# A transformer block in split float32 on one core: weight parts moved in the on-chip memory, and the products of the down-projection reordered

## The chip, the core and the metric

The kernel runs on one core of a Trainium2 chip. The core has TensorE (PE, matrix products, with its weight loads shown as PEld), VectorE (DVE), ScalarE (ACT), GpSimd (POOL) and SyncE (SP, which only issues DMAs). Each engine works off its own instructions in the order in which they were written into the program; between engines there are semaphores. The metric is the time of one execution in microseconds (us), the median of several runs.

## The reference, cut to what matters

One block over 512 tokens of width 2048. All weights and activations are float32.

```python
h    = rmsnorm(x, g_attn_pre)
proj = h @ w_in                               # q, k, v of 8 stick-breaking heads, latents of 8 MLA heads
o_sb, o_mla = stick_breaking(q, k, v), mla(latents, rope(positions))
x    = x + rmsnorm(concat(rmsnorm(o_sb), rmsnorm(o_mla)) @ w_o, g_attn_post)
h    = rmsnorm(x, g_ffn_pre)
u    = causal_depthwise_conv(h @ w_up)        # w_up 2048 x 11264, width 3
gate, val = split(u)
x    = x + rmsnorm((gelu(gate) * val) @ w_down, g_ffn_post)   # w_down 5632 x 2048
```

## The kernel before, in words

**Split products.** A float32 product is made from three products of rounded parts: each factor is split into a high part (a rounding cast, `hi`, made on ScalarE) and a low part (what is left, `lo`, a subtraction on VectorE), and `three` issues high by high, high by low and low by high. Weights go the same way: a raw tile `wr` is loaded by SP, ScalarE casts it to `wh`, VectorE subtracts to `wl` (L109 and L111 in the attention, `w_parts`, L921, in the feed-forward).

**Start.** `gen_v` (L305) makes the values first: for each block of weight rows it loads weights (`load_w`), loads and splits a block of x, and issues 12 matmuls a block. The first two blocks are loaded one at a time, the others in pairs, into two raw buffers. On VectorE the operations of `rope_tables` (the angles, sine and cosine by range reduction, L390 to L425) lie between those splits. Then comes the first query and key product, `qk0`; after 6 of its matmuls `bcast` (L145) spreads the row scales over the partitions with a float32 matmul of `t` (VectorE, L139) by `ones`.

**Feed-forward.** The columns of gate and value are taken in 22 units of 256 pairs. Unit 0 is done plainly (`plain_part`, L865). The other 21 use a scheme of seven products in place of eight on a 2 x 2 split of weights and activations (`sevenfold`): p1 loads the quarter w11, p5 needs w11 + w12 (an addition in place, `plus`, L925), p6 that + w22, p7 w12 + w22, p2 is w21, p3 w22, p4 w11 + w12 + w22 + w21. Each product of the up-projection is 48 matmuls of 256 columns (L984), 21 x 7 x 48 = 7056 in all. The parts have three buffers each (`w_pair`), the raw quarters four.

**Down-projection.** The 5632 rows of w_down go in five chunks of 1024 rows (four units), and the last 512 rows plainly (`last_steps`). A chunk has two halves of columns (q = 0, 1), and each half seven products of 24 matmuls of 512 columns (L1156), 5.4 us each. The left sides, sums of the gated activations split in two parts, are made by `g_side` (L1123 on ScalarE, L1124 and L1129 on VectorE): those of the next chunk product by product in the half q = 1, those of the first chunk at the end of the up-projection (`then`). In the traces the sides go by their pages: product 1 reads a6h, 2 a6l, 5 a3h, 6 s, 7 a3l, 3 and 4 act_lo. Products 1 and 2 share two PSUM banks X, 5 and 3 share D, 7 and 4 share C, 6 has Y. After product 1, X is added to the accumulator u2 (`add_to`, L1094; in the first chunk a copy on ScalarE, L1092), then product 2 adds on in X, and the sum goes to the accumulator "11". For p7 and p4 the raw sums are made by DMAs of GpSimd that accumulate (`added`). After the last chunk twelve operations combine the accumulators (L1219, L1223, L1224), and the plain rows are added to them bank by bank (`take`, L1243).

**What sets the order.** The main loop keeps two products' weights ahead: it makes the parts of the product after next, then issues a product. `ORDER` (L1159) and the order in which `sevenfold` returns its parts set the products of a half. A scheduler lays the operations of each engine out from that, and `issue_after` holds one back behind another. A pool of tiles takes addresses from a stack; a tile that takes the address of an older one waits for the older one's last reader.

Of the kernel before, what the change touches and what calls it, by code (L numbers as in the profile page):

```python
# [19 lines left out]
P = 128  # L20
# [29 lines left out]
def hymba_block(ctx, tc, x, xT, positions, vecs, taps, w_in, w_uq, w_ukv, w_o, g_attn_post, w_up, w_down,  # L50
# [22 lines left out]

    ident = const.tile([P, P], F32, name="ident")
# [3 lines left out]
    ones = const.tile([P, P], F32, name="ones")  # L78
    po.memset(ones, 1.0)
# [25 lines left out]
    def load_w(src, r0, kn, c0, cols):  # L105
        raw = new_raw([P, kn, cols])
# [198 lines left out]
    def gen_v(vb, first=False):  # L305
        banks = [bank() for _ in range(NT)]
        steps = [1, 1] + [2] * 7 if first else [2] * 8
        for kg, kn in enumerate(steps):
            k0 = sum(steps[:kg])
            wh, wl = load_w(w_in, k0 * P, kn, 2 * SBW + vb * 512, 512)  # L310
# [12 lines left out]
        for t in range(NT):  # L323
            hi, lo = pg_v(R32), pg_v(R32)
            sc.activation(hi, banks[t], AF.Copy, scale=rx[:, t:t + 1])
            ve.scalar_tensor_tensor(lo, banks[t], rx[:, t:t + 1], f(hi), ALU.mult, ALU.subtract)
            v_sb[vb].append((hi, lo))
# [54 lines left out]
    def rope_tables():  # L382
# [6 lines left out]
        with behind(("lo", 4)):  # L389
# [100 lines left out]
    run(qk0, 1.0)  # L490
# [423 lines left out]
    made = []  # L914

# [12 lines left out]
    def sevenfold(quarter, shape, added=None):  # L928
# [3 lines left out]
        def p1():  # L932
            pair = w_pair(*shape)
            if not made:
                wq.tile([P, 256], F32, tag="gap", name="gap", bufs=1)
# [30 lines left out]
        if added:  # L966
            return p1, p2, p5, p6, p7, p3, p4
# [22 lines left out]
    def up_steps(unit):  # L990
# [61 lines left out]
        def then(use, *ns):  # L1052
            def both(w):
                use(w)
                if ns[0] == 6:
# [6 lines left out]
        if unit == NFF // 2 - 1:  # L1062
            return zip(sevenfold(quarter, (8, 256)), (m1, m5, then(m6, 1), then(m7, 2), m2, then(m3, 5),
                                            then(m4, 6, 7, 3, 4)))
# [14 lines left out]
    def open_down():  # L1079
        some(len(later))  # L1080
        tp_stack.close()
        d["gp"], d["gpool"] = stacked("gp", side="right")
        d["rest"] = kept("act_lo", (16, S), R32)
# [75 lines left out]
    ORDER = (1, 2, 5, 6, 7, 3, 4)  # L1159

    def down_steps(ch, q):
# [16 lines left out]
        def use(n, w):  # L1178
# [5 lines left out]
            if q == 1 and ch + 1 < NST:  # L1184
                g_side(ch + 1, n)
            if n == 1:
# [18 lines left out]
    def open_last():  # L1205
# [9 lines left out]
        for t in range(2):  # L1215
            for q in range(2):
                y[t, q], u2 = acc["11"][t, q], acc["u2"][t, q]
                y[2 + t, q], y[t, 2 + q], y[2 + t, 2 + q] = acc["21"][t, q], acc["12"][t, q], acc["22"][t, q]
                ve.tensor_tensor(y[t, 2 + q], y[t, 2 + q], u2, ALU.subtract)  # L1219
        for t in range(2):  # L1220
            for q in range(2):
                u2 = acc["u2"][t, q]
                ve.tensor_tensor(y[2 + t, 2 + q], y[2 + t, 2 + q], u2, ALU.subtract)  # L1223
                ve.tensor_tensor(y[2 + t, q], y[2 + t, q], u2, ALU.add)  # L1224
# [132 lines left out]
```

## Time and profile before

| | us |
|---|---|
| median of 3 runs | 2044.94 (2043.98 to 2048.38) |
| profiled execution | 2040.72 |
| its span (first to last instruction) | 2038.9 |
| TensorE busy | 2003.2 |
| VectorE busy | 1532.6 |
| ScalarE busy | 924.4 |

The profile is of one execution. It lists what each engine was busy with, and for each idle stretch what ended it. Busy time of TensorE is 98% of the span, so the stretches of interest are those between its instructions. The chain that ended last runs over TensorE for 82% of the span.

### The profile page before, as it was taken

Reading aid. Unit: us, or ns where it says so; the run is one execution under the profiler, and the core shown is the slowest. Engines: PE = TensorE matmul, PEld = TensorE weight load, DVE = VectorE, ACT = ScalarE, POOL = GpSimd, SP = SyncE. Lnnn points to the kernel's source line nnn. Section 1 sums busy time; section 2 is a strip of 40 time slices with the busy share of each in tenths; the row PEclk is TensorE's granted clock in tenths of the full one; section 3 lists DMA queues with packets and bytes.
Section 4 is the critical chain, followed back from the end, with each engine's and each line's share of the span. In section 5 each row is a group of like instructions: output and inputs, shape, how many; then the busy total and the mean of one; then the engine's idle time right before and its main releaser. Section 6 shows DMA issues by size and latency. Waiting matters only on the chain.

```text
span 2038.9 us, 29849 instructions
## 1 busy us (share of the span) xinstructions
PE 2003.2 (98%) x12580; PEld 1808.4 (89%) x12580; DVE 1532.6 (75%) x1556; ACT 924.4 (45%) x1105; POOL 159.6 (8%) x192
## 2 busy tenths in 40 slices
PE   9999999999999999999999999999999999999997
PEld 7788888888888889999999999999999788878876
DVE  7454355687343888888888888888888889898886
ACT  6343244466433654454444444444444564444432
POOL 0000000123021200000000000000000000000004
PEclk9999999999999999999999999999999999999999
DMA  8422322211532524224323432343235677767772
GB/s 277 125 73 74 103 73 65 81 42 63 181 122 99 177 95 133 94 94 148 132 94 99 159 115 94 114 154 105 94 129 187 180 189 203 206 169 183 207 206 83
DMA packets 186630, 266.12 MB, mean 131 GB/s; under 512 B 8832, under 2 KB 123648, under 8 KB 185984
## 3 DMA queue, kind: packets, MB, share of 16 engines
q1 hardware_dynamic: 170704, 227.04, 34.2%
q0 software_dynamic: 15360, 36.71, 8.2%
q8 instruction: 98, 1.61, 0.3%
q10 hardware_dynamic: 432, 0.47, 0.1%
q14 instruction: 36, 0.29, 0.0%
HBM read 244.26 MB, written 19.92 MB: 130 GB/s over the span
## 4 chain that ended last, share of the span: by engine, by line
PE 82%; DVE 9%; DMA 3%; issue 3%; ACT 3%; POOL 0%; SPq 0%; DVEq 0%; ACTq 0%; POOLq 0%
PE ps L984 40%; PE ps L1156 10%; PE ps L120 9%; PE ps L121 9%; PE ps L122 9%; PE ps L270 2%; DVE wl L921 2%; ACT wh L921 1%; DMA wr<-in_w_down_dram 1%; PE ps L865 1%; DVE wr L925 1%; PE ps L246 1%; DVE act_hi L1094 1%; DVE t L452 0%; DVE wl L111 0%
## 5 line engine op out<-in xcount | busy, mean ns | idle before, releaser
L921 ACT CAST wh<-wr 128x2048 fp32r<-128x2048 f32 x220 | 419.0, 1909 | 613.5 <-DVE wr L925 274.1
L921 DVE TENSOR_TENSOR wl<-wr,wh 128x2048 fp32r<-128x2048 f32 x220 | 503.1, 2288 | 149.6 <-ACT wh L921 149.4
L984 PE MATMUL ps<-act_hi,wh 128*128 128x256 f32 x1344 | 380.4, 283 | 1.6 <-ACT wh L921 1.6
L984 PE MATMUL ps<-act_hi,wl 128*128 128x256 f32 x1344 | 380.4, 283 | 0.0
L984 PE MATMUL ps<-act_lo,wh 128*128 128x256 f32 x1344 | 380.4, 283 | 0.0
L111 DVE TENSOR_TENSOR wl<-wr,wh 128x1024 fp32r<-128x1024 f32 (+2 forms) x107 | 130.3, 1218 | 185.1 <-ACT wh L109 184.8
L984 PEld LDWEIGHTS ps<-act_hi,wh 128*128 128x128 f32 x1344 | 258.0, 192 | 1.9 <-ACT wh L921 1.8
L984 PEld LDWEIGHTS ps<-act_lo,wh 128*128 128x128 f32 x1344 | 258.0, 192 | 0.0
L984 PEld LDWEIGHTS ps<-act_hi,wl 128*128 128x128 f32 x1344 | 258.0, 192 | 0.0
L925 DVE TENSOR_TENSOR wr<-wr 128x2048 f32<-128x2048 f32 x104 | 237.7, 2286 | 1.1
L109 ACT CAST wh<-wr 128x1024 fp32r<-128x1024 f32 (+2 forms) x107 | 110.3, 1031 | 200.4 <-PE ps L121 78.3
L122 PE MATMUL ps<-wh,act_lo 128*128 128x512 f32 x400 | 156.2, 390 | 0.0
L120 PE MATMUL ps<-act_hi,wh 128*128 128x512 f32 x368 | 145.2, 395 | 0.0
L122 PE MATMUL ps<-act_hi,wl 128*128 128x512 f32 x368 | 143.4, 390 | 0.0
L121 PE MATMUL ps<-act_lo,wh 128*128 128x512 f32 x368 | 143.4, 390 | 0.0
L120 PE MATMUL ps<-wh,act_hi 128*128 128x512 f32 x352 | 138.1, 392 | 5.0 <-ACT act_hi L194 5.0
L121 PE MATMUL ps<-wl,act_hi 128*128 128x512 f32 x352 | 137.5, 391 | 0.0
L1156 PE MATMUL ps<-wh,act_lo 128*128 128x512 f32 x320 | 100.4, 389 | 0.7 <-ACT act_hi L1092 0.7
L984 PE MATMUL ps<-a5h,wl 128*128 128x256 f32 x336 | 95.2, 283 | 1.5 <-DVE wl L921 1.5
L984 PE MATMUL ps<-a6h,wl 128*128 128x256 f32 x336 | 95.1, 283 | 0.0
L984 PE MATMUL ps<-a5h,wh 128*128 128x256 f32 x336 | 95.1, 283 | 0.0
L984 PE MATMUL ps<-a3h,wh 128*128 128x256 f32 x336 | 95.1, 283 | 0.0
(392 smaller groups left out, 4351.9 us busy)
## 6 DMA issues: line engine op xcount, KB each, us to landing
wr<-in_w_up_dram SPq DMA_DIRECT2D x84, 1024.0 KB, 6.5
wr<-in_w_down_dram SPq DMA_DIRECT2D x44, 1024.0 KB, 6.9
wr<-in_w_in_dram SPq DMA_DIRECT2D x59, 512.0 KB, 3.7
wr<-in_w_down_dram POOLq DMA_DIRECT2D x20, 1024.0 KB, 9.7
wr<-in_w_o_dram SPq DMA_DIRECT2D x32, 512.0 KB, 3.6
g_dram<-v POOLq DMA_DIRECT2D x42, 256.0 KB, 6.0
a5l<-g_dram SPq DMA_DIRECT2D x5, 1024.0 KB, 11.0
a5h<-g_dram SPq DMA_DIRECT2D x5, 1024.0 KB, 8.3
```

The costliest lines, as they stand in the source:

```text
L109: sc.copy(hi, raw)
L111: ve.tensor_tensor(lo, raw, f(hi), ALU.subtract)
L120: te.matmul(ps, lh, rh, start=start, stop=False)
L121: te.matmul(ps, lh, rl, start=False, stop=False)
L122: seen["mm"] = te.matmul(ps, ll, rh, start=False, stop=stop)
L246: te.transpose(dst, a(b, j), ident)
L270: te.matmul(dst, q[:, b * P:(b + 1) * P], k[:, k0:S], start=i == 0, stop=False)
L865: mark["part"] = te.matmul(dst, l[:, kk, ms], r, start=first and kg == 0 and kk == 0 and i == 0, stop=kg == 3 and kk == 3 and i == 2, skip ...
L921: made.append((sc.copy(hi, w), ve.tensor_tensor(lo, w, f(hi), ALU.subtract)))
L925: ve.tensor_tensor(w, w, v, ALU.add)
L984: te.matmul(dst, l[:, k, ms], r[:, k, :], start=fresh and k == 0 and m == 0 and i == 0, stop=k == 7 and i == 2, skip_group_check=True)
L1156: te.matmul(bs[t], l[:, k, ts_], r[:, k, :], start=fresh and k == 0 and i == 0, stop=k == FU - 1 and i == 2, skip_group_check=True)
```

## The change

1. **Start.** `ones` is made first, and nine matmuls of `ones` by `ones` (128 columns) into an unused bank come ahead of everything on TensorE. The first four blocks of `gen_v` are loaded one at a time into pages that are free then ("s", "om"), not into the raw buffers. Rope's operations wait for the evacuation of the values, not for a split of x. `bcast` comes later in `qk0`.
2. **Addresses.** The raw quarters of the feed-forward are placed at the bottom of their pool, 71 to 103 KB of each partition, the high parts at 103 to 127, the low parts at 127 to 151; before, the high parts lay at 71 to 95, the low at 95 to 119, and the raw quarters at 120 to 152 KB.
3. **Passage.** The left sides of the first chunk: 1, 5 and 2 are made at the products 6, 7 and 3 of the last up unit, 6, 7, 3 and 4 behind the products 1, 5, 2 and 6 of the first down half (before: 1, 2, 5 at 6, 7, 3, and the other four behind 4).
4. **Order.** The down-projection's products go 1, 5, 2, 6, 7, 3, 4 (before 1, 2, 5, 6, 7, 3, 4), their parts likewise.
5. **End.** The twelve combining operations are held behind the last split of a weight.

```diff
+    ones = const.tile([P, P], F32, name="ones")
+    po.memset(ones, 1.0)
+    idle = bank()
+    for _ in range(9):
+        te.matmul(idle[:, 0:P], ones, ones, start=True, stop=True)
...
-        steps = [1, 1] + [2] * 7 if first else [2] * 8
+        steps = [1] * 4 + [2] * 6 if first else [2] * 8
...
-            wh, wl = load_w(w_in, k0 * P, kn, 2 * SBW + vb * 512, 512)
+            raw = page("s" if kg < 2 else "om", 3).rearrange("p (k c) -> p k c", k=1) if kn == 1 else None
+            wh, wl = load_w(w_in, k0 * P, kn, 2 * SBW + vb * 512, 512, raw)
...
-        with behind(("lo", 4)):
+        with behind("v"):
             ve.tensor_copy(ang, posi)
...
-    run(qk0, 1.0)
+    run(qk0, 7.7)
...
     made = []
+    wq.tile([P, 8, 256], F32, tag="wr", name="wr", bufs=4)
...
-            if not made:
-                wq.tile([P, 256], F32, tag="gap", name="gap", bufs=1)
...
         if added:
-            return p1, p2, p5, p6, p7, p3, p4
+            return p1, p5, p2, p6, p7, p3, p4
...
-            return zip(sevenfold(quarter, (8, 256)), (m1, m5, then(m6, 1), then(m7, 2), m2, then(m3, 5),
-                                            then(m4, 6, 7, 3, 4)))
+            return zip(sevenfold(quarter, (8, 256)), (m1, m5, then(m6, 1), then(m7, 5), m2, then(m3, 2),
+                                            then(m4)))
...
-    ORDER = (1, 2, 5, 6, 7, 3, 4)
+    ORDER = (1, 5, 2, 6, 7, 3, 4)
...
+            if first and q == 0:
+                {1: open_sixth, 5: lambda: g_side(0, 7), 2: lambda: g_side(0, 3),
+                 6: lambda: g_side(0, 4)}.get(n, lambda: None)()
...
-        for t in range(2):
-            for q in range(2):
...
+        with tc.issue_after(made[-1][1].ins):
+            for t in range(2):
+                for q in range(2):
```

How the instructions stand shows at three places. In the changed file the lines are three to ten higher.

VectorE ahead of the broadcast, before: L139 makes `t`, L481 and L126 the sums and scales that it needs, L111 is a low weight part, L390 to L425 are rope.

```order
L408 SCALAR_TENSOR_TENSOR aT<-aT 128x512 x5
L419 TENSOR_TENSOR aT<-aT 128x512
L481 TENSOR_REDUCE ssr<-ssx 128x4
L403 TENSOR_SCALAR aT<-aT 128x512
L126 TENSOR_SCALAR ms<-ssr 128x4
L404 TENSOR_SCALAR aT<-aT 128x512
L485 TENSOR_SCALAR sx<-rs 128x4
L486 TENSOR_SCALAR nsx<-rs 128x4
L139 TENSOR_TENSOR t<-ident,rs 128x512
```

And after (L142 is `t`, L114 a low weight part, L330 the evacuation of the values, L394 the first operation of rope):

```order
L489 TENSOR_SCALAR sx_492<-rs_490 128x4
L490 TENSOR_SCALAR nsx_493<-rs_490 128x4
L142 TENSOR_TENSOR t_512<-ident_87,rs_490 128x512
L114 TENSOR_TENSOR wl_520<-wr_516,wh_518 128x1024
L114 TENSOR_TENSOR wl_550<-wr_546,wh_548 128x1024
L330 SCALAR_TENSOR_TENSOR v_497<-ps_118,rs_490,v_496 128x512
L114 TENSOR_TENSOR wl_633<-wr_629,wh_631 128x1024
L330 SCALAR_TENSOR_TENSOR v_501<-ps_119,rs_490,v_500 128x512
L114 TENSOR_TENSOR wl_663<-wr_659,wh_661 128x1024
L330 SCALAR_TENSOR_TENSOR v_505<-ps_120,rs_490,v_504 128x512
L330 SCALAR_TENSOR_TENSOR v_509<-ps_121,rs_490,v_508 128x512
L394 CAST aT_570<-posi_568 128x512
```

All of rope has moved behind the values (L330), and nothing of it stands ahead of `t`.

SP at the entry into the feed-forward, before: the loads of the last plain weights (L107) and the first raw quarters (L994), with what each waits for.

```order
L107 DMA wr_5982<-in_w_up_dram 128x4x256 [waits DMAHW1_49,DMAHW7_49,DVE_49,Activation_49]
L994 DMA wr_6250<-in_w_up_dram 128x8x256 [waits DMASW3_49,DMASW5_49,DMASW2_49,DMAHW2_49,DMASW0_49,Activation_49]
L994 DMA wr_6254<-in_w_up_dram 128x8x256 [waits DMAHW3_49,Activation_49,Pool_49]
L994 DMA wr_6273<-in_w_up_dram 128x8x256 [waits DMAHW4_49,DVE_49,PE_49]
L994 DMA wr_6385<-in_w_up_dram 128x8x256 [waits DMAHW5_49,PE_49]
```

And after:

```order
L110 DMA wr_5998<-in_w_up_dram 128x4x256 [waits DMAHW0_49,DMAHW2_49,DVE_49,Activation_49]
L997 DMA wr_6266<-in_w_up_dram 128x8x256 [waits DMAHW3_49,PE_49]
L997 DMA wr_6270<-in_w_up_dram 128x8x256 [waits DMAHW4_49,DVE_49,PE_49]
L997 DMA wr_6289<-in_w_up_dram 128x8x256 [waits DMAHW5_49]
L997 DMA wr_6401<-in_w_up_dram 128x8x256 [waits DMAHW6_49,Activation_49]
```

The first and the second raw quarter have come to wait for TensorE (PE): the second for the last matmul of the plain product, the third stands right behind it.

VectorE in the half of the down-projection that begins at 1747 us, before: L921 are low parts (of product 2, then 5), L925 the additions for 5 and 6, L1094 the additions to accumulators (the first pair on the names ps_16018 and ps_16019 is product 1), L1124 and L1129 left sides.

```order
L921 TENSOR_TENSOR wl_15977<-wr_15974,wh_15976 128x2048
L1124 TENSOR_TENSOR act_lo_14970<-a5h_15769,act_lo_14970 128x512
L1124 TENSOR_TENSOR act_lo_14970<-a5l_15770,act_lo_14970 128x512
L1094 TENSOR_TENSOR v_14974<-v_14974,ps_15901 128x512
L1094 TENSOR_TENSOR v_14975<-v_14975,ps_15902 128x512
L925 TENSOR_TENSOR wr_15938<-wr_15938,wr_16010 128x2048
L1094 TENSOR_TENSOR act_hi_14971<-act_hi_14971,ps_16018 128x512
L1094 TENSOR_TENSOR act_hi_14971<-act_hi_14971,ps_16019 128x512
L921 TENSOR_TENSOR wl_16015<-wr_15938,wh_16014 128x2048
L1129 TENSOR_TENSOR a5h_16274<-a5h_16274 128x2x256
L925 TENSOR_TENSOR wr_15938<-wr_15938,wr_16046 128x2048
```

And after (L926 low parts, of product 5, then 2; L930 the additions, L1100 those to accumulators, ps_16034 and ps_16035 product 1):

```order
L930 TENSOR_TENSOR wr_15954<-wr_15954,wr_15990 128x2048
L1130 TENSOR_TENSOR act_lo_14969<-a5h_15785,act_lo_14969 128x512
L1100 TENSOR_TENSOR v_14973<-v_14973,ps_15917 128x512
L1100 TENSOR_TENSOR v_14974<-v_14974,ps_15918 128x512
L926 TENSOR_TENSOR wl_15995<-wr_15954,wh_15994 128x2048
L1130 TENSOR_TENSOR act_lo_14969<-a5l_15786,act_lo_14969 128x512
L926 TENSOR_TENSOR wl_16031<-wr_16028,wh_16030 128x2048
L1100 TENSOR_TENSOR act_hi_14970<-act_hi_14970,ps_16034 128x512
L1100 TENSOR_TENSOR act_hi_14970<-act_hi_14970,ps_16035 128x512
L930 TENSOR_TENSOR wr_15954<-wr_15954,wr_16062 128x2048
```

The addition and the low part for product 5 have moved ahead of the low part of product 2 and of the additions of product 1.

## Rows read from the trace of the kernel before

**Rows 1.** The page: busy time of each engine, its share of the span, instructions.
```profile
PE 2003.2 (98%) x12580; PEld 1808.4 (89%) x12580; DVE 1532.6 (75%) x1556; ACT 924.4 (45%) x1105; POOL 159.6 (8%) x192
```
**Rows 2.** Waits of TensorE: line, what it waited for, us in total, times, longest.
```profile
PE ps L1156 <- DVE act_hi L1094: 5.0, 6, 1.1
PE ps L1156 <- DVE wl L921: 5.0, 2, 2.9
```
**Rows 3.** Timeline of TensorE, first matmuls: start, duration, operation [idle before <- released by].
```profile
5.03 0.79 PE L120 MATMUL ps<-wh,act_hi 128*128 128x512 f32 x1 [5.03 <-ACT act_hi L194]
...
7.33 0.63 PE L122 MATMUL ps<-wh,act_lo 128*128 128x512 f32 x1
7.76 0.54 PE L120 MATMUL ps<-wh,act_hi 128*128 128x512 f32 x1
```
**Rows 4.** Timeline of TensorE at the broadcast of the row scales.
```profile
53.30 1.10 PE L145 MATMUL ps<-t,ones 128*128 128x512 f32 x2 [1.54 <-DVE t L139]
...
54.46 0.39 PE L121 MATMUL ps<-act_lo,wh 128*128 128x512 f32 x1
```
**Rows 5.** Timeline of VectorE ahead of the broadcast.
```profile
52.47 0.69 DVE L139 TENSOR_TENSOR t<-ident,rs 128x512 f32<-128x512 f32 x1
```
**Rows 6.** Timeline of TensorE at the entry into the feed-forward.
```profile
737.41 0.39 PE L865 MATMUL ps<-act_hi,wl 128*128 128x512 f32 x1
...
745.25 0.39 PE L984 MATMUL ps<-a5h,wl 128*128 128x256 f32 x1 [1.46 <-DVE wl L921]
...
752.90 0.39 PE L984 MATMUL ps<-act_hi,wh 128*128 128x256 f32 x1 [1.63 <-ACT wh L921]
```
**Rows 7.** Line L994, its two loads issued at 732.6 and 733.1.
```profile
DMA to landing us min/median/max: 5.3/7.1/9.0
```
**Rows 8.** Timeline of VectorE at the entry.
```profile
738.64 2.28 DVE L925 TENSOR_TENSOR wr<-wr 128x2048 f32<-128x2048 f32 x1
...
750.78 4.48 DVE L921 TENSOR_TENSOR wl<-wr,wh 128x2048 fp32r<-128x2048 f32 x2
```
**Rows 9.** Timeline of TensorE in the first half of the down-projection.
```profile
1595.01 0.50 PE L1156 MATMUL ps<-wh,a6l 128*128 128x512 f32 x1 [0.98 <-ACT act_hi L1092]
...
1603.62 0.50 PE L1156 MATMUL ps<-wl,a3h 128*128 128x512 f32 x1 [2.87 <-DVE wl L921]
```
**Rows 10.** Timeline of VectorE there.
```profile
1601.29 2.28 DVE L921 TENSOR_TENSOR wl<-wr,wh 128x2048 fp32r<-128x2048 f32 x1
```
**Rows 11.** Timeline of TensorE in two halves of the down-projection.
```profile
1752.13 0.39 PE L1156 MATMUL ps<-wh,a6h 128*128 128x512 f32 x1
1753.63 0.47 PE L1156 MATMUL ps<-wh,a6l 128*128 128x512 f32 x1 [1.11 <-DVE act_hi L1094]
...
1764.84 0.39 PE L1156 MATMUL ps<-wl,s 128*128 128x512 f32 x1
1765.06 0.39 PE L1156 MATMUL ps<-wh,s 128*128 128x512 f32 x1
...
1951.06 0.49 PE L1156 MATMUL ps<-wl,a3h 128*128 128x512 f32 x1 [2.16 <-DVE wl L921]
```
**Rows 12.** Stretch: length, busy time of each engine (instructions), clock, DMA share, GB/s.
```profile
1680.00:1760.00 80.00, 78.89 (x348) 64.81 (x347) 73.45 (x73) 35.76 (x32) 5.13 (x4) 1.00 0.73 210
```
**Rows 13.** Timeline of VectorE in the half that begins at 1747.
```profile
1752.80 1.28 DVE L1094 TENSOR_TENSOR act_hi<-act_hi,ps 128x512 f32<-128x512 f32 x2
1754.94 2.29 DVE L921 TENSOR_TENSOR wl<-wr,wh 128x2048 fp32r<-128x2048 f32 x1 [0.86 <-ACT wh L921]
...
1762.16 2.29 DVE L921 TENSOR_TENSOR wl<-wr,wh 128x2048 fp32r<-128x2048 f32 x1 [0.26 <-ACT wh L921]
```
**Rows 14.** Timeline of VectorE in the last rows.
```profile
2028.30 0.69 DVE L1243 TENSOR_TENSOR act_hi<-ps,act_hi 128x512 f32<-128x512 f32 x1 [2.03 <-PE ps L122]
```
**Rows 15.** Groups by line and shape: count, busy us, mean ns, idle before.
```profile
L984 PE MATMUL ps<-act_hi,wl 128*128 128x256 f32 x1344 | 380.4, 283 | 0.0
L865 PE MATMUL ps<-act_lo,wh 128*128 128x256 f32 x64 | 18.1, 283 | 0.0
```

More of the change, by code (lines that the diff above doesn't have):

```diff
@@ L77, in hymba_block @@
     po.tensor_copy(identb, ident)
-    ones = const.tile([P, P], F32, name="ones")
-    po.memset(ones, 1.0)
     sbmask = const.tile([P, P], BF16, name="sbmask")
@@ L103, in new_raw, with load_w @@
         return wp.tile(shape, F32, tag="wr", name="wr", bufs=2)
-    def load_w(src, r0, kn, c0, cols):
-        raw = new_raw([P, kn, cols])
+    def load_w(src, r0, kn, c0, cols, raw=None):
+        raw = new_raw([P, kn, cols]) if raw is None else raw
         sy.dma_start(raw, src[r0:r0 + kn * P, c0:c0 + cols].rearrange("(k p) c -> p k c", p=P))
@@ L325, in gen_v @@
             sc.activation(hi, banks[t], AF.Copy, scale=rx[:, t:t + 1])
-            ve.scalar_tensor_tensor(lo, banks[t], rx[:, t:t + 1], f(hi), ALU.mult, ALU.subtract)
+            seen["v"] = ve.scalar_tensor_tensor(lo, banks[t], rx[:, t:t + 1], f(hi), ALU.mult, ALU.subtract)
             v_sb[vb].append((hi, lo))
@@ L1054, in both @@
                 use(w)
-                if ns[0] == 6:
+                if not ns:
                     open_down()
@@ L1077, in kept, with open_sixth @@
         return hp.tile([P, *shape], dt, tag=name, name=name)
-    def open_down():
+    def open_sixth():
         some(len(later))
@@ L1082, in open_down @@
         d["gp"], d["gpool"] = stacked("gp", side="right")
+        g_side(0, 6)
+    def open_down():
         d["rest"] = kept("act_lo", (16, S), R32)
@@ L1214, in open_last @@
         acc = d["acc"]
-        for t in range(2):
-            for q in range(2):
[L1217 to L1224, printed above, removed]
+        with tc.issue_after(made[-1][1].ins):
+            for t in range(2):
+                for q in range(2):
+                    y[t, q], u2 = acc["11"][t, q], acc["u2"][t, q]
+                    y[2 + t, q], y[t, 2 + q], y[2 + t, 2 + q] = acc["21"][t, q], acc["12"][t, q], acc["22"][t, q]
+                    ve.tensor_tensor(y[t, 2 + q], y[t, 2 + q], u2, ALU.subtract)
+            for t in range(2):
+                for q in range(2):
+                    u2 = acc["u2"][t, q]
+                    ve.tensor_tensor(y[2 + t, 2 + q], y[2 + t, 2 + q], u2, ALU.subtract)
+                    ve.tensor_tensor(y[2 + t, q], y[2 + t, q], u2, ALU.add)
         d["ssy"] = sm.tile([P, NT, 8], F32, tag="ssy", name="ssy", bufs=2)
```

## The prediction

> **What bounds the kernel now.** I read the page's busy lines first: TensorE is busy 2003.2 of 2038.9 us [rows 1], so a change that leaves its work alone can win only in its idle stretches. The waits of TensorE by releaser, read next, say who ends them: six times, 5.0 us together, product 2 of the down-projection waits for an addition of VectorE, and twice, 5.0 us together, for a low weight part [rows 2]. The timeline of TensorE then gives the places: the start [rows 3], the broadcast of the row scales [rows 4], the entry into the feed-forward [rows 6], the passage from up- to down-projection [rows 9], and the down halves [rows 11]. A wait costs a little more than its bracket: at 1752.13 stands the last matmul of product 1, a step is 0.23, and the next starts at 1753.63, so 1.27 are lost where 1.11 are shown [rows 11]; I add 0.16 to each. VectorE is second: in the down-projection it is busy 73.45 of 80 us, against 78.89 of TensorE [rows 12].
>
> **The start.** The first matmul waits for its data until 5.03; it and the five behind it are spaced 0.43 (7.33 to 7.76) [rows 3], those of the same size later 0.22 to 0.23 (1764.84 to 1765.06) [rows 11]. So 6 x 0.20 = 1.2 us are lost to TensorE's lower level, 1.2 GHz, which it leaves once it has worked for a while (the spacing shows this, the clock lines of the page do not). The change puts nine matmuls of 128 columns into the empty time ahead. One of 512 columns of this float32 kind took 1.16 - 0.23 = 0.93 (53.30 to 54.46, less one common matmul) [rows 4]; a quarter of it, doubled at the lower level, is 0.47, and nine are 4.2 us. From about 1 us on they end at about 5.2, as the data come: **-1.2**, between +0.3 (they end late and the level is not reached) and -1.4.
>
> The Trainium skill ("TensorE: Matmul & The Clock Gate", Part 1) says that the default state is throttled, that activity releases it, and that the same kernel shows different counts of cold matmuls from run to run. By that rule the saving would be anything from nothing to the 1.2 us in a given run; one trace cannot show it.
>
> The broadcast waits for t of VectorE, 1.54 + 0.16 = 1.7 us [rows 4]. VectorE makes t at 52.47 [rows 5], with rope's operations ahead of it. Afterwards rope stands behind the evacuation of the values, and TensorE has 36 matmuls of the first query product ahead of the broadcast instead of 6, 30 x 0.23 = 6.9 us of cover: **-1.7**, between 0 and -1.7. If that cover were gone (the query weights, queued behind all sixteen row loads of x, come late), the 1.7 would stay. The four single loads of the first blocks take SP out of the wait for a raw buffer; no wait for a weight stands among TensorE's up to 53.30, so they are costed at nothing.
>
> **Entry into the feed-forward.** Raw weights move onto what the last plain product still reads. The order of SP shows that the second raw load (needed for product 5) now waits for that product's last matmul, at 737.41 [rows 6]; before, VectorE's addition alone was late. A load of this size landed in 5.3 us when first of a pair, in 9.0 when second [rows 7]. So it lands at 737.7 + 5.3 = 743.0. From the start of the addition to TensorE's resumption were 745.25 - 738.64 = 6.6 us (addition, cast, low part) [rows 6, 8]: TensorE resumes at 749.6, **+4.4**. A little comes back at the next wait, 1.63 before product 6 [rows 6]: from the end of one low part (TensorE's release at 745.25) to the start of the next at 750.78 lie 5.5 us, of which two additions take 2 x 2.28 [rows 6, 8]; the other 0.9 is small work that VectorE will have done while it waits: **-0.9**. The third load, second of the pair, lands at 738.2 + 9.0 = 747.2, in time for 749.6. Together +3.5, between +2.8 (the wait of 1.63 goes as a whole) and, if the needed load takes 9.0, +7.2. The order of the rest of the up-projection stays, and the addresses of the parts are priced at nothing (a rival below).
>
> **From up to down.** Two waits go. Product 2 waited 0.98 for the copy of product 1's banks, since both use one pair of banks [rows 9]; with product 5 between them the copy has 5.4 us: -1.1. Product 5 waited 2.87 for its low part [rows 9], which VectorE ran at 1601.29 behind left-side work [rows 10]; the change hands those sides out one per product, behind that part: -3.0. Sum **-4.1**, between -1.1 (the low part is still late) and -4.1. The later small waits there I leave.
>
> **The down halves.** The six waits of product 2 are 5.0 + 6 x 0.16 = 6.0 us [rows 2]; product 5 between gives VectorE 5.4 us for 1.3 us of additions. The wait for the low part at 1951.06, 2.16 + 0.16 = 2.3 [rows 11], goes too: the constant products that stood ahead of it on VectorE are moved behind the last split. That is -8.3. Does product 5 now come too early for its own weights? In the half from 1747, its low part ends at 1754.94 + 2.29 = 1757.23 [rows 13]. In the new order the part of product 2 (2.29) and the two additions (1.28) stand behind it, and the 0.86 for which VectorE idled ahead of it is filled: 1757.23 - 4.43 = 1752.8. TensorE wants it at its third matmul, 1752.13 + 3 x 0.23 = 1752.8: just in time. Product 6 has 1765.06 - (1762.16 + 2.29) = 0.6 us in hand [rows 11, 13], and will be wanted 1.27 earlier, so it may wait 0 to 0.7. Three halves look like this (the longer waits of 1.1 stand there): I take 3 x 0.33 = +1.0. Sum **-7.3**, between 0 (VectorE takes all back) and -8.3.
>
> **The end.** The twelve constant products, about 0.6 us each by an addition of that size (two take 1.28 [rows 13]), 7.7 us in all, now stand together ahead of the first addition of the last rows. TensorE writes on in other banks meanwhile, and VectorE still waited 2.03 for it before the very last addition [rows 14], so that it catches up: 0, up to +3 if the banks run out.
>
> **Sum.** -1.2 - 1.7 + 3.5 - 4.1 - 7.3 = -10.8. The profiled execution took 2040.72 (span 2038.9, 1.8 around it), which gives 2029.9; the median of the runs is 2044.94, 4.2 above, and measured against it the forecast is 2034.1.
>
> **Rivals.**
> 1. VectorE is the bound of the down-projection. At 92% busy in a fixed order, every wait taken from the additions returns at a low part (0 for the halves, -1.1 for the passage): -1.2 - 1.7 + 3.5 - 1.1 = -0.5, 2044.4. For it: 73.45 of 80, and margins of 0.6 [rows 12, 13]. Against it: TensorE's work alone leaves it 78.89 - 73.45 = 5.4 us per 80, more than the 2 us of waits per 80 that go.
> 2. Slower: product 5 misses its weights. If its chain does not move ahead (its load or cast keeps its old time), it is 1757.23 - 1752.8 = 4.4 late in each of the three tight halves, and in the first, where it had nothing in hand [rows 9], by a whole product, 24 x 0.227 = 5.4: +18.6, less the waits that go. 3 x 4.4 + 5.4 - 8.3 - 4.1 + 0.6 = +6.8, where 0.6 is the start and the entry (-2.9 + 3.5): 2051.7. It is slower than before by more than 4.1 from 4.0 us late in each of the four on; the new order of VectorE, with the addition for product 5 ahead of the part of 2, speaks against it.
> 3. Address matters to TensorE's reading. Each ns on the 7056 matmuls of the up-projection is 7.1 us, so the forecast turns slower by over 4.1 from 2.1 ns on; 3 ns give +10.4, 2055.3, and 3 ns the other way 2012.9. Against it: in the plain product and in the later ones, with parts at other addresses, a matmul of 256 columns takes 283 ns alike [rows 15].
> 4. The entry costs nothing, because the load lands early or its wait is hidden: 2030.6.
>
> The Trainium skill ("SBUF — State Buffer", Who interferes with whom) has only the port pair that VectorE and GpSimd share as a point of contention, and TensorE waiting on nobody. By it rival 3 has no mechanism; here no run has had the parts at the new addresses.
>
> **Chances.** Forecast 0.58, rival 1 0.24, rival 2 0.07, rival 3 0.05 (half of it slower), rival 4 0.06. What a measurement can tell from no change is 0.2%, 4.1 us: faster means under 2040.9, slower over 2049.0. Of the forecast's 0.58 a tenth stays within that (0.06), of rival 1 an eighth falls below (0.03). Faster: 0.52 + 0.03 + 0.02 + 0.06 = 0.63; slower: 0.07 + 0.03 = 0.10; same 0.27. Range 2029 (all lower bounds) to 2047 (rival 1 with the entry at +6).
>
> **What the changed profile would show.** First matmuls spaced 0.23 from about 5 us; no wait before the broadcast; a wait of 5 to 6 us, not 1.5, for the low part of product 5 at the entry, and a shorter one for product 6; no waits of product 2 for an addition in the halves. Waits for low parts in the halves of over 1 us each would show rival 1 or 2; up-projection matmuls of other than 283 ns rival 3.

## The result

The changed kernel takes 2033.21 us (median of 4 runs, 2033.05 to 2034.04), the kernel before 2044.46 us (4 runs); the ratio is 0.994, with a 95% interval of 0.9925 to 0.996. So it is 0.58% faster, 11.3 us, where 10.8 had been forecast. The two profiled executions are only 7.5 us apart (spans 2038.94 and 2031.46). Why both numbers hold is the main point below. One of the ten executions in experiment two took 3304.89 us at a granted clock of 0.556 and is left out of its numbers.

The busy lines and the waits of TensorE after the change (line waited for: us in total, times, longest); lines are three to ten higher than before.

```profile
PE 2005.8 (99%) x12598; PEld 1814.6 (89%) x12598; DVE 1533.4 (75%) x1557; ACT 924.9 (46%) x1106; POOL 159.8 (8%) x192
```

```profile
PE ps L987 <- ACT wh L926: 4.0, 1, 4.0
PE ps L1162 <- DVE wl L926: 3.1, 4, 1.7
PE ps L987 <- DVE wl L926: 1.8, 1, 1.8
PE ps L148 <- DVE t L142: 1.7, 1, 1.7
```

The six waits for an addition [rows 2] are gone, and so is the first of the two broadcast waits [rows 4]; what is left of L148 is the second broadcast, which the change does not touch. New are 4.0 + 1.8 us at the entry and four waits, 3.1 us, for low parts in the down-projection.

The most useful table is the start of the same matmul in both profiles, since TensorE's list of work is nearly the same. I give what the changed kernel stands ahead (-) or behind (+):

| place | before | after | ahead or behind | gained here | forecast |
|---|---|---|---|---|---|
| second broadcast | 403.48 | 401.05 | -2.43 | -2.4 | -2.9 |
| last plain matmul | 737.41 | 735.22 | -2.19 | +0.2 | 0 |
| last of the up-projection | 1587.84 | 1590.69 | +2.85 | +5.0 | +3.5 |
| last product of the first half | 1627.85 | 1624.61 | -3.24 | -6.1 | -4.1 |
| last matmul | 2027.87 | 2019.29 | -8.58 | -5.3 | -7.3 |
| end of the span | 2038.94 | 2031.46 | -7.48 | +1.1 | 0 |

Three of the terms hide something: the start, the entry and the halves.

**The entry, after.** VectorE's addition for product 5, which starts as the load lands; TensorE's timeline at that product; and stretches around it (length, busy time of each engine, clock, DMA share, GB/s):

```profile
741.12 2.29 DVE L930 TENSOR_TENSOR wr<-wr 128x2048 f32<-128x2048 f32 x1 [4.58 <-DMA wr<-in_w_up_dram]
```

```profile
745.40 0.39 PE L987 MATMUL ps<-a5h,wh 128*128 128x256 f32 x1 [4.03 <-ACT wh L926]
747.72 0.58 PE L987 MATMUL ps<-a5h,wl 128*128 128x256 f32 x1 [1.82 <-DVE wl L926]
748.10 0.41 PE L987 MATMUL ps<-a5h,wh 128*128 128x256 f32 x1
748.32 0.41 PE L987 MATMUL ps<-a5l,wh 128*128 128x256 f32 x1
```

```profile
735.00:741.00 6.00, 6.00 (x50) 5.92 (x49) 0.75 (x1) 3.85 (x5) 0.00 (x0) 1.00 0.73 232
741.00:747.70 6.70, 0.87 (x6) 0.46 (x4) 6.53 (x6) 2.38 (x2) 0.58 (x1) 0.88 0.93 301
747.70:753.00 5.30, 5.28 (x25) 5.28 (x26) 5.30 (x4) 1.90 (x1) 0.54 (x1) 0.51 0.10 36
753.00:758.00 5.00, 5.00 (x43) 5.00 (x43) 5.00 (x4) 3.82 (x2) 0.00 (x0) 1.00 0.06 19
```

TensorE stood idle for most of 6.7 us, and for the 5.3 us after that the granted clock is 0.51, the lower level of 1.2 GHz: 25 matmuls run there where the next 5 us hold 43. These matmuls take about 2 us longer, but little of it is paid: product 6 would have waited in any case. In the kernel before it resumes 7.65 us after product 5 does (745.25 to 752.90) [rows 6], and in experiment four's execution, where fewer matmuls ran slow, it is 7.66:

```profile
747.94 0.58 PE L987 MATMUL ps<-a5h,wl 128*128 128x256 f32 x1 [1.53 <-DVE wl L926]
755.60 0.39 PE L987 MATMUL ps<-act_hi,wh 128*128 128x256 f32 x1 [0.39 <-ACT wh L926]
```

In the changed kernel the slow matmuls fill that time, so that no wait of product 6 is left. Product 7 starts 13.89 us after product 5 resumes (761.61) and 13.51 before (758.76): the clock costs 0.4 us net.

**The halves, after.** VectorE in the half that begins at 1744:

```profile
1752.93 0.69 DVE L1135 TENSOR_TENSOR a5h<-a5h 128x512 f32<-128x512 f32 x1
1753.56 1.36 DVE L1100 TENSOR_TENSOR act_hi<-act_hi,ps 128x512 f32<-128x512 f32 x2
1757.70 0.69 DVE L1135 TENSOR_TENSOR a5l<-a5l 128x512 f32<-128x512 f32 x1 [2.78 <-DMA a5l<-g_dram]
1758.31 4.49 DVE L926 TENSOR_TENSOR wl<-wr,wh 128x2048 fp32r<-128x2048 f32 x2
```

The low part of product 6 (L926 at 1758.31) comes late, and TensorE waits for it at 1760.65. But VectorE was not full: it stood 2.78 us idle with that low part second in its queue, behind a subtraction for a left side of the next chunk (L1135), which waited for a load.

### The profile page after: what moved, and what is told of

Its sections match the earlier page's. It is cut to its first block, busy times and chain, and to the rows that moved or that the text cites. A ratio compares the mean times of both kernels' runs of the same rounds, so it can differ in the third digit from the quotient of the medians.

```text
span 2031.5 us, 29904 instructions
## 1 busy us (share of the span) xinstructions
PE 2005.8 (99%) x12598; PEld 1814.6 (89%) x12598; DVE 1533.4 (75%) x1557; ACT 924.9 (46%) x1106; POOL 159.8 (8%) x192
## 3 DMA queue, kind: packets, MB, share of 16 engines
q8 instruction: 99, 1.62, 0.3%
## 4 chain that ended last, share of the span: by engine, by line
PE 82%; DVE 8%; issue 4%; DMA 3%; ACT 2%; POOL 1%; SPq 0%; DVEq 0%; POOLq 0%; ACTq 0%
PE ps L987 42%; PE ps L1162 10%; PE ps L123 9%; PE ps L125 9%; PE ps L124 9%; PE ps L273 2%; DVE wl L926 2%; PE ps L869 1%; DVE act_hi L1100 1%; DMA wr<-in_w_down_dram 1%; DVE wr L930 1%; PE ps L249 1%; ACT wh L926 1%; DMA wr<-in_w_in_dram 1%; DMA acc<-in_x_dram 0%
## 5 line engine op out<-in xcount | busy, mean ns | idle before, releaser
L926 ACT CAST wh<-wr 128x2048 fp32r<-128x2048 f32 x220 | 419.0, 1908 | 586.3 <-DVE wr L930 280.8
L926 DVE TENSOR_TENSOR wl<-wr,wh 128x2048 fp32r<-128x2048 f32 x220 | 502.8, 2287 | 146.5 <-ACT wh L926 146.2
L114 DVE TENSOR_TENSOR wl<-wr,wh 128x1024 fp32r<-128x1024 f32 (+1 forms) x104 | 127.8, 1229 | 170.8 <-ACT wh L112 170.6
L930 DVE TENSOR_TENSOR wr<-wr 128x2048 f32<-128x2048 f32 x104 | 237.6, 2285 | 5.4 <-DMA wr<-in_w_up_dram 4.6
L112 ACT CAST wh<-wr 128x1024 fp32r<-128x1024 f32 (+1 forms) x104 | 108.1, 1039 | 193.4 <-PE ps L125 70.6
L987 PE MATMUL ps<-a5l,wh 128*128 128x256 f32 x336 | 96.1, 286 | 0.0
```

The costliest lines, as they stand in the source:

```text
L112: sc.copy(hi, raw)
L114: ve.tensor_tensor(lo, raw, f(hi), ALU.subtract)
L926: made.append((sc.copy(hi, w), ve.tensor_tensor(lo, w, f(hi), ALU.subtract)))
L930: ve.tensor_tensor(w, w, v, ALU.add)
L987: te.matmul(dst, l[:, k, ms], r[:, k, :], start=fresh and k == 0 and m == 0 and i == 0, stop=k == 7 and i == 2, skip_group_check=True)
```

## The experiments

All times are medians of the runs on one chip at a time; the kernel before stood at 2042.9 to 2043.7 beside them. "Over" and "under the changed kernel" mean against 2033.21; run again on the third chip, it took 2033.58.

**One: the addresses undone.**

```diff
-    wq.tile([P, 8, 256], F32, tag="wr", name="wr", bufs=4)
...
+            if not made:
+                wq.tile([P, 256], F32, tag="gap", name="gap", bufs=1)
```

> The changed kernel with one part undone: the raw quarters of the feed-forward lie above the high and low parts again, as before. Theory (the entry costs 5.0 us because the second raw load waits for the last plain matmul): the wait for product 5 at the entry falls from 4.0 + 1.8 back to about 1.5 + 1.6, everything behind stands 5.0 earlier, and the time is 2033.2 - 5.0 = 2028.2. Rival (the addresses pay somewhere later, in the up-projection or the halves): the entry gets shorter, but less than 5.0 arrives at the end, 2030 to 2033.

Measured: 2030.64 (2030.11 to 2031.34), 2.6 under the changed kernel, half of what the theory wanted. The entry is 2.9 us shorter, not 5.0; its waits:

```profile
737.65 0.39 PE L988 MATMUL ps<-act_hi,wl 128*128 128x256 f32 x1 [2.21 <-DVE wl L925]
744.77 0.39 PE L988 MATMUL ps<-a5h,wl 128*128 128x256 f32 x1 [1.13 <-DVE wl L925]
752.42 0.39 PE L988 MATMUL ps<-act_hi,wh 128*128 128x256 f32 x1 [1.63 <-ACT wh L925]
```

The first wait is new: the low part of the first product now falls on the place of the last plain low part. Which buffer the last plain weights lie in depends on how many buffers were taken up before, and the start takes another number. So the old addresses are not free here either, 2.1 us dearer than before at the entry (plain end to up-projection end), against 5.0 with the new ones. No gain or loss arrives later in the up-projection, where the distance to the kernel before stays as it is to 0.01 us. At the last matmul this execution is 3.5 ahead of the changed kernel; the last steps (experiment six) then take 13.1 us instead of 12.2.

**Two: the addresses alone, on the kernel before.**

```diff
+    wq.tile([P, 8, 256], F32, tag="wr", name="wr", bufs=4)
...
-            if not made:
-                wq.tile([P, 256], F32, tag="gap", name="gap", bufs=1)
```

> The kernel before with one part of the change: the raw quarters at the bottom, the parts above. Here the first raw quarter, not the second, falls on a place that is read late, as in the kernel with the start undone. Theory (addresses count only through waits at the entry): +4 at the entry, the matmuls of the up-projection at 283 ns and 0.12 apart as before, 2042.9 + 4 = 2047. Rival (address matters to TensorE's reading or to other transfers): a difference spread over the 850 us of the up-projection or the halves.

Measured: 2048.04 (nine runs, 2045.32 to 2050.54), ratio to before 1.0021 (1.0011 to 1.003), so 4.4 us slower. Here the first product waits 2.0 + 1.8; the entry costs 4.0 (plain end to up-projection end), and from 758 to 1593 the distance to the kernel before does not change. The matmuls of the up-projection keep their duration:

```profile
L984 PE MATMUL ps<-act_lo,wh 128*128 128x256 f32 x1344 | 380.9, 283 | 0.0
```

The profiled execution, a slower one of 2050.39, also loses 4.5 us in the halves; the kernel before loses 2.0 there in its second profile (experiment ten), in part at the same waits. So in the up-projection an address costs nothing in itself; it costs by whose place a load must wait for. For the halves this run alone cannot tell; in experiment five TensorE runs them at the new addresses without a wait, 1667 matmuls in 377.6 us, 0.227 each as in the kernel before.

**Three: another load for the late place.** In the first unit w21, needed last but two, is loaded ahead of w12, and by GpSimd, so that SP does not stand behind its wait.

```diff
             w[11] = quarter(0, 0)
+            if not made:
+                w[21] = quarter(1, 0, po)
...
         def p2():
-            w[21] = quarter(1, 0)
+            if 21 not in w:
+                w[21] = quarter(1, 0)
...
```

> The changed kernel with one thing moved: for the first unit with seven products the load of w21 (needed only by the fifth product) is issued by GpSimd ahead of that of w12, so that w21 and not w12 gets the place that the last plain matmul still reads. Theory (the entry costs what it does because the load that product 5 needs waits for that place): the waits at the entry, 4.0 + 1.8 in the changed kernel, fall to about 1, and the time is 7 us below that of the changed kernel, about 2026. Rival (at the entry ScalarE and VectorE, with the work of the plain unit, are the bound): the load comes early, but product 5 still waits 3 or more, 2029 or above.

Measured: 2028.53 (2028.3 to 2028.81), 4.7 under the changed kernel. The waits at the entry are those of the kernel before, to the hundredth [rows 6]:

```profile
743.10 0.39 PE L990 MATMUL ps<-a5h,wl 128*128 128x256 f32 x1 [1.46 <-DVE wl L926]
...
750.75 0.39 PE L990 MATMUL ps<-act_hi,wh 128*128 128x256 f32 x1 [1.63 <-ACT wh L926]
```

From the last plain matmul to the end of the up-projection it takes 850.42 us again, as before, so the entry's whole price came from the late load. What is left, which the theory put at 1 us, is 3.1. Of it the 1.46 stands behind the plain unit's convolution: the addition for product 5 is on VectorE behind one of its operations, which waits for ScalarE, which waits for one of the last plain matmuls. It stood there in the kernel before too.

**Four: the order undone** (products and parts 1, 2, 5, 6, 7, 3, 4).

```diff
-            return p1, p5, p2, p6, p7, p3, p4
+            return p1, p2, p5, p6, p7, p3, p4
...
-    ORDER = (1, 5, 2, 6, 7, 3, 4)
+    ORDER = (1, 2, 5, 6, 7, 3, 4)
```

> The changed kernel with one part undone: products and parts of the down-projection in the order 1, 2, 5, 6, 7, 3, 4 again. Theory (the order hides the additions of product 1): the six waits of product 2, 6.0 us, and that of the first half, 1.1, come back; the waits for low parts that the changed kernel shows there (0.95, 1.83, 0.49, 0.49, 3.8 together) go: +3.3, 2036.5. Rival (VectorE is the bound in the halves, so that the order only moves the waits): 2033 within 1.

Measured: 2035.76 (2034.47 to 2036.91), 2.6 over the changed kernel, between the theory and the rival. The additions' waits return:

```profile
PE ps L1162 <- DVE act_hi L1100: 4.2, 4, 1.1
```

Four of them come back, not six, and no wait for a low part of over 0.2 us is left. The order is worth some 2 to 3 us net: it removes waits of product 2 and gives part of that back at products 5 and 6. In the first half nothing comes back, not even the wait of product 2 (1.1) that the theory wanted there: the passage keeps its gain of 6 us without the order, so that gain is from the spread sides.

**Five: the left-side subtraction held back.**

```diff
         def sub(o, u, v):
-            for i in range(2):
-                ve.tensor_tensor(o[i], u[i], v[i], ALU.subtract)
+            late = tc.issue_after(made[147 + 14 * (ch - 1) + 3][1].ins) if ch and n == 5 else ExitStack()
+            with late:
+                for i in range(2):
+                    ve.tensor_tensor(o[i], u[i], v[i], ALU.subtract)
```

> The changed kernel with one thing added: the subtraction for the left side of product 5 of the next chunk, which the changed kernel runs in the half before and which waited 2.8 and 2.0 us there for a load, is held behind the low part of product 6. Theory (product 6 waits because its low part stands in VectorE's queue behind that subtraction, not because VectorE is full): the waits 0.95 and 1.83 of product 6 go, 2033.2 - 2.8 = 2030.4. Rival (VectorE is full): the same time comes back at another low part, 2033 within 0.5.

Measured: 2028.73 (2028.17 to 2030.09), 4.5 under the changed kernel, more than the 2.8 of the theory. All four waits for low parts in the halves are gone, those of product 5 too, and the halves from the end of the up-projection on are 4.4 shorter. VectorE does the same work (1534.8 us busy against 1533.4) and is not the bound; that rival falls.

**Six: the combining operations held less far back**, behind the low part of product 6 of the last half.

```diff
-        with tc.issue_after(made[-1][1].ins):
+        with tc.issue_after(made[-8][1].ins):
```

> The changed kernel with one number changed: the twelve combining operations are held behind the low part of product 6 of the last half, not behind the last split, so that they may run in VectorE's idle stretches of that half. Theory (the time from the last matmul to the end grew from 11.0 to 12.2 us because VectorE comes late into the last rows): 11.0 again and no new wait in the last half, 1.2 below the changed kernel, about 2032. Rival (the 1.2 is of another cause, such as the DMA of the result): no change.

Measured: 2032.34 (2031.99 to 2033.88), 0.9 under the changed kernel, whose runs overlap with these (2033.05 to 2034.04); the profiles tell more. No new wait stands in the last half, and the time from the last matmul to the end is 11.5 us, where it was 12.2 in the changed kernel and 11.1 in the kernel before. The last steps on GpSimd (POOL) and VectorE in the changed kernel, and then in this one:

```profile
2019.71 0.69 DVE L1253 TENSOR_TENSOR act_hi<-ps,act_hi 128x512 f32<-128x512 f32 x1 [0.43 <-PE ps L125]
2020.80 1.27 POOL L1286 TENSOR_TENSOR v<-v,a3h 128x512 f32<-128x512 f32 x1
2021.26 1.36 DVE L1286 TENSOR_TENSOR act_hi<-act_hi,a3h 128x512 f32<-128x512 f32 x1 [0.85 <-ACT v L1254]
```

```profile
2018.51 1.27 POOL L1286 TENSOR_TENSOR v<-v,a3h 128x512 f32<-128x512 f32 x1
2019.06 0.69 DVE L1253 TENSOR_TENSOR act_hi<-ps,act_hi 128x512 f32<-128x512 f32 x1 [2.03 <-PE ps L125]
2020.60 0.69 DVE L1286 TENSOR_TENSOR act_hi<-act_hi,a3h 128x512 f32<-128x512 f32 x1 [0.85 <-ACT v L1254]
```

With all twelve in one lump VectorE has only just caught up by the last bank: it has 0.43 in hand instead of 2.03, and the addition itself (L1253) still starts 0.4 after the last matmul, as before. But GpSimd's products come behind VectorE's earlier additions and are late. The last of them now runs beside VectorE's product by the gain (L1286), which takes 1.36 instead of 0.69. These 0.67 us come back in this run. The other 0.43 stays: it lies behind the last operation of VectorE, in the writing of the result, which took 4.35 us in the profile of the kernel before and 4.78 in that of the changed one. It is 4.34 to 4.36 in the profiles of experiments three, seven, nine and eleven, though they keep most of the change, and 4.77 to 4.79 in the others of the changed kernel, so the change does not set it, and what does is not shown; the rival has this part.

**Seven: the start undone.**

```diff
-    run(qk0, 7.7)
+    run(qk0, 1.0)
...
-        steps = [1] * 4 + [2] * 6 if first else [2] * 8
+        steps = [1, 1] + [2] * 7 if first else [2] * 8
```

(and the nine matmuls, the pages of the first blocks and the place of rope likewise)

> The changed kernel with the start undone: no matmuls ahead, first blocks loaded as before, rope between the splits, the broadcast after 6 matmuls. Theory (2.4 us of the gain come from the start, as the times of the same matmul at 400 us show): 2035.6, first matmuls spaced 0.43 and a wait of 1.5 ahead of the broadcast. Rival (part of the start's gain is the clock, which differs from run to run): single runs spread by over 1 us and the median lies anywhere from 2033.5 to 2036.

Measured: 2036.74 over 10 runs from 2034.31 to 2041.46, 3.5 over the changed kernel. In its profile 14 of the first matmuls are slow (0.42 us or more to the next), against 6 in the profile of before, with the same code up to there. Undoing the start also moves the late place at the entry: the first raw quarter gets it, as in experiment two, and the entry costs 4.0 us instead of 5.0. At the second broadcast this execution is 4.0 behind the changed kernel (405.06 against 401.05), so the 3.5 are somewhat less than the start is worth in it.

**Eight: without the nine matmuls.**

```diff
-    idle = bank()
-    for _ in range(9):
-        te.matmul(idle[:, 0:P], ones, ones, start=True, stop=True)
```

> The changed kernel without the nine matmuls ahead. Theory (at the start the first 6 to 14 real matmuls run at the lower level, differently from run to run, 0.2 us each): 1.2 to 2.8 us above the changed kernel, and single runs spread by 1.5 us or more. Rival (the first matmuls wait for data anyway, so that the lower level costs nothing): the same time as the changed kernel.

Measured: 2035.39 (2034.77 to 2036.2), 2.2 over the changed kernel; the first 11 matmuls start 0.42 or more apart, and the second broadcast is 1.6 later (402.69). With the matmuls ahead, in the changed kernel, all but the first are spaced 0.23:

```profile
0.98 4.21 PE L78 MATMUL ps<-ones 128*128 128x128 f32 x18 [0.98 <-POOL ones L75]
5.19 0.59 PE L123 MATMUL ps<-wh,act_hi 128*128 128x512 f32 x1
5.62 0.39 PE L124 MATMUL ps<-wl,act_hi 128*128 128x512 f32 x1
5.85 0.39 PE L123 MATMUL ps<-wh,act_hi 128*128 128x512 f32 x1
```

The spread without them is narrow, 1.4, so the spread of single runs is not the clock's alone.

**Nine: the nine matmuls alone**, with the rest of the start undone.

> The changed kernel with the start undone, but with the nine matmuls ahead kept. Theory (the spread of single runs comes from the count of slow first matmuls): 1 to 2 us below the kernel with the whole start undone (2036.7), runs within 2 us of each other; the rest of the start's gain, the 1.7 of the broadcast, is missing. Rival (the spread comes from loads that hold up the blocks, not from the clock): single runs spread as widely as there, by 5 us or more.

Measured: 2039.59 over 11 runs from 2035.64 to 2040.73, spread by 5.1: by the medians 2.9 dearer than with the whole start undone, though the two sets of runs overlap. TensorE begins faster and then stands at the first query weights:

```profile
52.69 0.52 PE L123 MATMUL ps<-act_hi,wh 128*128 128x512 f32 x1 [3.08 <-ACT wh L112]
55.03 0.80 PE L125 MATMUL ps<-act_hi,wl 128*128 128x512 f32 x1 [1.40 <-DVE wl L114]
```

The cast waits for the load. So the nine matmuls gained 2.2 us with the loads ahead (experiment eight) and nothing here. Why this is dearer than without them is not shown. The theory that the spread comes from the count of slow matmuls falls.

**Ten: the kernel before once more.**

> The kernel before once more, for a second profile, since the first stood 3 to 4 us under the median of its runs. Theory (what differs from run to run lies in the first 150 us: slow first matmuls and late blocks): the same matmul at 145 us comes later in a slower execution, and everything after runs alike. Rival (the difference lies in the down-projection, where VectorE leaves little slack): the waits there differ.

Measured: 2044.27 over 11 runs (2040.82 to 2047.93), and a profile with a span of 2045.3, 6.4 us longer than the first one. Of these, 3.8 are there by the second broadcast (407.25 against 403.48), nearly all at the first broadcast. TensorE there, and stretches around it; then VectorE's wait and the same place in the changed kernel:

```profile
55.42 1.21 PE L145 MATMUL ps<-t,ones 128*128 128x512 f32 x2 [3.53 <-DVE t L139]
55.95 1.10 PE L120 MATMUL ps<-act_hi,wh 128*128 128x512 f32 x1
56.85 0.63 PE L121 MATMUL ps<-act_lo,wh 128*128 128x512 f32 x1
```

```profile
51.50:55.40 3.90, 0.39 (x2) 0.01 (x1) 1.94 (x8) 2.24 (x4) 1.12 (x1) 1.00 0.52 168
55.40:59.60 4.20, 4.18 (x10) 3.01 (x11) 4.17 (x6) 2.45 (x3) 0.00 (x0) 0.60 0.30 81
```

```profile
52.53 0.18 DVE L481 TENSOR_REDUCE ssr<-ssx 128x4 f32<-128x16 f32 x1 [1.50 <-ACT acc L201]
```

```profile
46.23 0.18 DVE L485 TENSOR_REDUCE ssr<-ssx 128x4 f32<-128x16 f32 x1 [13.13 <-ACT acc L204]
```

In the slower execution the sum behind `t` waits for the last squares of x, hence for the last row loads of x, not for rope. The wait at the broadcast is 3.53 instead of 1.54, and the clock falls behind it (0.60), so that 8 matmuls run at half speed: 2.0 + 1.6 us. In the first profile of the kernel before the two stood level, rope's last operation ahead of the sum ending at 50.41 and the last squares at 50.38:

```profile
49.72 0.69 DVE L419 TENSOR_TENSOR aT<-aT 128x512 f32<-128x512 f32 x1
50.41 0.18 DVE L481 TENSOR_REDUCE ssr<-ssx 128x4 f32<-128x16 f32 x1
```

```profile
50.20 0.18 ACT L201 ACTIVATION_READ_ACCUMULATOR acc<-acc 128x1 f32 x1
```

In the changed kernel SP has issued the last row load of x by 40.9 us (before 46.5), the loads run at 363 GB/s from 5 to 20 us where the kernel before had 272, and the sum comes at 46.23.

Of the other 2.6 us, 0.6 are there by the last plain matmul and 2.0 come in the halves. There the same wait has another price: product 5 of the first half waited 2.87 us in the first profile [rows 9] and 2.90 in this one (to 1607.98), and behind it the granted clock was 1.00 there and 0.50 here:

```profile
1605.30:1608.20 2.90, 2.90 (x14) 2.39 (x14) 1.52 (x3) 2.27 (x2) 0.00 (x0) 1.00 0.80 329
```

```profile
1609.60:1612.50 2.90, 2.90 (x8) 2.30 (x7) 1.63 (x3) 2.22 (x2) 0.00 (x0) 0.50 0.86 353
```

In the last half two waits (1.63 and 0.70) are again followed by 8 matmuls at half speed, which cost 1.55 us. So the theory and the rival have a part each.

**Eleven: the three mends together** (three, five and six).

> The changed kernel with the three mends together: w21 of the first unit loaded by GpSimd into the place that is read late, the left-side subtraction held behind product 6's low part, the combining operations held behind that of the last half. Theory (the three stretches are apart, TensorE is the bound in between): 2033.2 - 4.7 - 4.5 - 0.9 = 2023.1. Rival (once the waits are gone VectorE or the loads are the next bound): the gains don't add, 2026 or above.

Measured: 2024.08 (2023.45 to 2024.22), ratio to before 0.9902 (0.9888 to 0.9915). That is 9.1 us under the changed kernel where the sum wanted 10.1, so the gains nearly add up. The waits of over 1 us that are left are known by place: 1.5 and 1.6 at the entry, 1.7 at the second broadcast.

**Twelve: the changed kernel once more.**

> The changed kernel once more, beside the three mends on the same chip: 2033 within 1.5, and beside the kernel before the same ratio as at first, 0.994 to 0.995. Its profile shows which of its waits return in the same place: the entry's 4.0 and 1.8, product 6's 0.8 and 1.7.

Measured: 2033.58 (2033.04 to 2035.44), ratio 0.995, span 2031.8. Every place of the table above lies within 0.35 us of the first profile of it.

## Why the prediction was right, and where it was not

**The number.** The forecast of -10.8 came out as -11.3, and in part that is luck. The sum was made against an execution at the short end: 2040.72, where half of the 66 runs of the kernel before lie from 2042.4 to 2045.2. I carried the 4.2 us between that profile and the median over to the changed kernel, as if they lay in something untouched. As far as the profiles show, they lie in places that the change rewrites. The four profiles with the old start reach the second broadcast at 403.48, 404.60, 405.06 and 407.25, the eight with the whole new start at 400.81 to 402.02. And the waits in the halves [rows 9, 11], which the change removes, were followed by matmuls at half speed in the profiles of experiments two and ten, but not in the first. The changed kernel's profile (2033.29) is within 0.1 of its median. Against the profile of before the sum was 3.3 us too good. The two errors cancelled; the step that failed is the last one of the sum.

**The start** (-2.9, measured -2.4 against the first profile, -6.2 against the second one, by the second broadcast). Two mechanisms were right: the matmuls ahead, which took 4.2 us as forecast, remove all but one of the slow first ones, and the broadcast has cover. The Trainium skill's rule ("TensorE: Matmul & The Clock Gate", Part 1, that the count of cold matmuls differs from run to run) is borne out: 6, 7, 8, 11 and 14 of the first matmuls start 0.42 us or more apart in the five profiles without the matmuls ahead. Incomplete was rope as the cause of a late `t`: the last row loads held it as long in the first profile and longer in the second. The first blocks' loads, which I costed at nothing, bring them early: from 5 to 20 us the nine profiles with single loads into free pages have 352 to 365 GB/s, the five with the old loads 268 to 286.

**The entry** (+3.5, measured +5.0). The place of the wait, the load behind it and the chain of 6.6 us from addition to resumption (741.12 to 747.72) were as forecast. Three terms were mis-sized. The addition began 5.9 us after the start of the last plain matmul instead of 5.6 (+0.3). The -0.9 at product 6 did not come: the small work that VectorE was to do while it waits stands behind product 5's low part in its queue (two operations of the convolution, at 747.59 and 750.44), so product 6's weights come as long after product 5 resumes as before. And the wait lets the clock fall, which the sum left out; it costs 0.4 net, since most of its 2 us fall into product 6's wait. I had the row for that price, the slow first matmuls [rows 3], and did not apply it to a wait that I made longer myself.

**The passage** (-4.1, measured -6.1). Both waits went (1.3 and 3.2), but the first not by the path that I gave: with the order undone (experiment four) product 2 does not wait there either, so it was not product 5 in between that gave the copy its time, but the spread sides. The two small ones that I left in the sum, 0.7 and 1.0, went too. Of the second I read in the traces that ScalarE's copy stood behind a cast that waited for a load (the cast at 1621.63 before, at 1616.31 after); no run separates the two.

**The halves** (-7.3, measured -5.3). The waits for additions went, and the low part at 1951 too. "Product 6 may wait 0 to 0.7" was the term: it waited 0.8 and 1.7, and product 5 0.3 twice. Against the second profile of the kernel before the halves gained 7.4, for the clock fell there. The cause was not the one I priced. I summed VectorE's work up to the low part and found it to fit, and it did fit; what broke it was one operation ahead in the queue that waits for a load. Rival 1 (VectorE is the bound) is refuted by experiment five.

**The end** (0, measured +1.1, within its bound). VectorE caught up, as forecast, but only by the last bank, and GpSimd did not: 0.67 are VectorE's product beside GpSimd's (experiment six). The other 0.43 is in the writing of the result and not of the change.

**Rivals 2 to 4.** Product 5 was late by 0.3 us at most in the first profile of the changed kernel and by 0.5 in the second, not by 4. Address has no price of its own in the up-projection (experiment two), as the Trainium skill ("SBUF — State Buffer", Who interferes with whom), by which TensorE waits on nobody, would have it. Rival 4 did not happen by itself, but experiment three shows how it would have looked: with another load in the late place the entry costs what it cost before.

## What to carry to other kernels

Before you add the gap between a profiled execution and the median to a forecast, find out where the gap lies: if it lies in a stretch that the change rewrites, it goes with it. When you move work ahead on an engine that works in order, sum its busy time up to the deadline, but also look for the one instruction ahead that waits for a load: it holds up everything behind it, however much slack the engine has. And when you give memory to a new owner, ask of each load who reads the place last, and let the load that is needed last have the place that is read last.

## What the runs showed of the hardware

- A wait of TensorE of 5.8 us (4.03 + 1.82) was followed by 5.3 us at a granted clock of 0.51, some 2 us on top; one of 3.53 was followed by 8 matmuls at half speed. Waits of 1.5 us in the same places [rows 4, 6] had no such price. The length of the wait alone does not tell: of two waits at the same matmul, 2.87 us was followed by a granted clock of 1.00 and 2.90 in another execution by 0.50 (experiment ten). Six executions of the changed kernel or a variant with the same late load had 12 to 22 slow matmuls at the entry, 1.1 to 2.1 us.
- A product of two tiles on VectorE took 0.69 us alone (experiment six) and up to 1.62 beside GpSimd at the same kind of operation (the changed kernel):

```profile
L1286 DVE TENSOR_TENSOR act_hi<-act_hi,a3h x4: 887/1248/1618, 1991.3 to 2021.3; 128x512 f32<-128x512 f32 x4
```

The columns are minimum, median and maximum in ns; with the combining operations held less far back the three are 692, 693 and 812. The Trainium skill ("SBUF — State Buffer", SBUF: two separate sides) says that VectorE and GpSimd share one pair of ports under an exclusive lock, where whoever comes second waits; VectorE's product at 2021.26 began second and ended at 2022.62, 0.55 after GpSimd's (2020.80 + 1.27), which agrees.
